# A pair's softmax issued one map of one head at a time, and a second gate group without set units

## The chip, the cores and the metric

The kernel runs on one core of one Trainium2 chip. The metric is the device time of one execution in microseconds. The kernel before took 1107.42 us, the median of 3 runs.

## The reference, cut to what matters

One layer on 256 tokens with 2048 features, all in float32. The input is normalised, multiplied by a wide matrix `w_in`, and the columns of the product feed two token mixers: gated linear attention (4 heads) and differential attention (16 heads with two softmax maps each). Both results are gated, sent through a branch matrix, merged, and projected out.

```python
h = rmsnorm(x, pre_norm_g[l])
proj = h @ w_in[l]                      # 2048 x (many columns)
(a_q, a_k, a_v, a_g, a_lr, b_q, b_k, b_v, b_g, m_a, m_b) = jnp.split(proj, offsets, axis=-1)
...
o_a = rmsnorm(gla_chunked(a_q, a_k, a_v, gk), gla_norm_g[l]) * silu(a_g)     # 4 heads, 512 wide
y_a = o_a @ w_branch_a[l]
...
# differential attention, per head: two maps of 256 x 256
s = jnp.einsum('bqhmd,bkhmd->bhmqk', qi, k)
p = jax.nn.softmax(jnp.where(mask, s, -jnp.inf), axis=-1)
w = p[:, :, 0] - lam * p[:, :, 1]
o = jnp.einsum('bhqk,bkhv->bqhv', w, v)
...
y_b = (rmsnorm(o_b, diff_norm_g[l]) * (1.0 - lam_init) * silu(b_g)) @ w_branch_b[l]
merged = sigmoid(m_a) * y_a + sigmoid(m_b) * y_b
x = x + rmsnorm(merged @ w_out[l], post_norm_g[l])
```

## The kernel before, in words

**Weights.** All weight matrices are cut into units of 128x1024 float32 (0.5 MB). A unit is loaded into one of 6 buffers called `raw`, or into a long-lived buffer called `chain` in which the POOL queue's DMAs add a second block of weights onto the first. ACT then writes a rounded copy `hi` (L341, for set units L304), DVE writes the rest `lo = raw - hi` (L342, L305), and PE multiplies: x's high part with hi, x's low part with hi, x's high part with lo. There are 3 `hi` and 3 `lo` buffers, and ACT and DVE prepare a unit up to `AHEAD = 4` steps before PE takes it.

**Set units and regular units.** Nine pairs of column groups are computed together as seven products in place of eight (p1, q3, p5, p2, q6, q7, p4; each of 4 units). These 9 x 28 = 252 units are the set units: 6 matmuls each at L712. When the product p5 is complete, ACT copies its PSUM bank into the tile `p` (L729) before the next product, q6, may write on in that bank. Everything else is regular: a unit of a gate group (`ag0` to `ag3` belong to the gated linear attention) has 12 matmuls at L512, a half of a channel chunk (`dq`, `dk`: queries and keys of the differential attention) has 16 at L533 and L535.

**The order of the steps** is written by hand in `schedule()`. `regular(keys)` appends the units of those column groups alone; `mixed(n, keys)` spreads n set units evenly between them. So `mixed(6, "ag2")` puts 6 set units among the 8 units of the third gate group, and `mixed(26, *channels(0))` puts 26 among the 16 units of the first four differential heads, which is called the first head stage. The group `m12` near the end is a merge gate with 14 set units.

**Background work.** Small work is written as generators, which `pump()` advances by one step: after a unit of some groups, after a channel chunk, and after every second set unit. `gla_out(hf, gates)` computes the output of two linear-attention heads: it fetches the values of the next head (`fetch_values`, L994, tiles `vh` and `vl`, from device memory on the SP queue), multiplies (9 matmuls per head at L494), normalises, and transposes. `diff_attention()` treats the 16 differential heads in 8 pairs. For a pair, `pair_scores` writes the scores of both heads and both maps into four PSUM banks. `exponents` then does one head: four masked maxima on DVE (L1041), one multiply that scales them (L1042), four exponentials on ACT (L1047). `diff_weights` joins the two maps, and later steps transpose the weights, apply them to the values, and normalise. DVE and ACT run these instructions in one order with the splits into hi and lo.

In the trace the trailing numbers and digits of the names are cut: `raw_ag` is a raw unit of any gate group, `raw_dq` and `raw_dk` of a channel chunk, `raw_s` of a set unit that is loaded plainly, `bg` a PSUM bank of background work, `set` one of a set product, `mm` one of a regular unit.

Of the kernel before, what the change touches and what calls it, by code (L numbers as in the profile page):

```python
# [10 lines left out]
AF = mybir.ActivationFunctionType  # L11
ALU = mybir.AluOpType
AX = mybir.AxisListType

P = 128
# [12 lines left out]
CUTS = ((0, P), (P, 3 * P))  # L28
# [47 lines left out]
def units(kind):  # L76
    return 2 * KT // ROWS[kind]


def schedule():  # L80

    kinds = {key: kind for key, kind, _, _ in chunk_plan()}
    steps = []
    blocks = [(i, n) for i in range(len(SETS)) for n in range(SLOTS * 4)]

    def regular(*keys):
        steps.extend((key, n) for key in keys for n in range(units(kinds[key])))

    def mixed(n, *keys):
        at = len(steps)  # L90
        regular(*keys)
        r = steps[at:]
        del steps[at:]
        for i, step in enumerate(r):
            steps.extend(blocks[: (i + 1) * n // len(r) - i * n // len(r)])
            del blocks[: (i + 1) * n // len(r) - i * n // len(r)]
            steps.append(step)

    def channels(g):
        return [key for key in kinds if key[:2] in ("dq", "dk") and key[2] == str(g)]  # L100

    order = [key for key, _, _, _ in chunk_plan()]
    def alone(n):
        steps.extend(blocks[:n])
        del blocks[:n]

    regular(*order[: order.index("v4")])
    mixed(SLOTS * 4, *order[order.index("v4") : order.index("ag0")])
    regular("ag0")
    mixed(4, "ag1")  # L110
    mixed(6, "ag2")
    mixed(26, *channels(0))
    mixed(28, *channels(1))
    mixed(28, *channels(2))
    mixed(28, *channels(3))
    mixed(14, "m12")
    mixed(42, *(f"y0{g}" for g in range(4)))
    alone(4)
    mixed(16, "y10", "y11")
    regular("y12", "y13")  # L120
    mixed(SLOTS * 4, "o2")
    regular("o3")
    assert not blocks
    return steps
# [41 lines left out]
def hybrid_kernel(ctx: ExitStack, tc, xt, xn, preg, postg, w, w2, gkb, glag, lamv, diffg, ident_d, causal_d, lmask_d, out):  # L166
    nc = tc.nc
    pe, act, dve, pool, sp = nc.tensor, nc.scalar, nc.vector, nc.gpsimd, nc.sync
# [14 lines left out]
    def sm(shape, name, dtype=F32, bufs=2):  # L183
        count[0] += 1
        return small.tile(shape, dtype, tag=name, name=f"{name}_{count[0]}", bufs=bufs)

    def t2(shape, name):
        count[0] += 1
        return small.tile(shape, F32, tag="t2", name=f"{name}_{count[0]}", bufs=8)

    def ps(tag):
        count[0] += 1
        return psum.tile([P, 512], F32, tag="bank", name=f"{tag}_{count[0]}")
# [5 lines left out]
    def f32(ap):  # L199
        return ap.bitcast(F32)  # L200


    steps = schedule()
    kinds, sizes, begins = {}, {}, {}
    off = 0
# [226 lines left out]
    neg_scale = const.tile([P, 2, 2], F32, name="neg_scale")  # L432
    score_scale = const.tile([P, 2], F32, name="score_scale")
# [392 lines left out]
    for g, n in enumerate(VG[2:]):  # L826
        banks = token_major(f"v{g + 2}", n, x_ops, 2)
# [169 lines left out]
    for g in range(3):  # L997
# [3 lines left out]
        banks = token_major(f"ag{g}", 512, x_ops)  # L1001
# [19 lines left out]
    def pair_scores(g, pair, qk):  # L1021
        banks = [[ps("bg"), ps("bg")] for _ in range(2)]
        for b in range(2):
            lo, up = CUTS[b]
            t, n = slice(P * b, P * b + P), up - lo
            for i2 in range(2):
                for m in range(2):
                    r = slice(64 * m, 64 * m + 64)
                    pe.matmul(banks[i2][m][:, lo:up], qk[r, 0, i2, t], qk[r, 1, i2, :n], start=True, stop=True)
        return [{"g": g, "pair": pair, "h": 2 * pair + i2, "banks": banks[i2]} for i2 in range(2)]  # L1030

    def exponents(s):
        cm = causal.rearrange("p a t -> p (a t)")
        prob = [t2([P, 384], f"prob{m}") for m in range(2)]
        mx = sm([P, 4], "mx", bufs=3)
        z = sm([P, 4], "z", bufs=4)
        banks = s["banks"]
        for m in range(2):
            for b in range(2):
                lo, up = CUTS[b]  # L1040
                dve.tensor_tensor_reduce(out=prob[m][:, lo:up], in0=banks[m][:, lo:up], in1=cm[:, lo:up], scale=1.0, scalar=-3e38, op0=ALU.add, op1=ALU.max, accum_out=mx[:, 2 * m + b : 2 * m + b + 1])  # L1041
        dve.tensor_tensor(out=mx, in0=mx, in1=neg_scale.rearrange("p m b -> p (m b)"), op=ALU.mult)  # L1042
        for m in range(2):
            for b in range(2):
                lo, up = CUTS[b]
                i = 2 * m + b
                act.activation(prob[m][:, lo:up], prob[m][:, lo:up], AF.Exp, scale=score_scale[:, b : b + 1], bias=mx[:, i : i + 1], accum_out=z[:, i : i + 1])  # L1047
        s.update(z=z, prob=prob)

    def diff_weights(s):  # L1050
        z, prob = s["z"], s["prob"]
        c = sm([P, 2], "c", bufs=2)
        dve.reciprocal(out=c, in_=z[:, 2:4])
        dve.scalar_tensor_tensor(out=c, in0=z[:, 0:2], scalar=neg_lam, in1=c, op0=ALU.mult, op1=ALU.mult)
        for b in range(2):
            lo, up = CUTS[b]
            dve.scalar_tensor_tensor(out=prob[0][:, lo:up], in0=prob[1][:, lo:up], scalar=c[:, b : b + 1], in1=prob[0][:, lo:up], op0=ALU.mult, op1=ALU.add)

    def turn_weights(s):
        bank = ps("bg")  # L1060
        for i in range(3):
            pe.transpose(bank[:, P * i : P * i + P], s["prob"][0][:, P * i : P * i + P], ident)  # L1062
        s["bank"] = bank
# [23 lines left out]
    def diff_attention():  # L1087

        last = pair = og = None
        n = 0  # L1090
        while "out1" not in done:
            yield
        while n < 16 or last or pair:
            new = None
            if n < 16:
                if n % 2 == 0:
                    while not waiting or f"pair{waiting[0][0]}{waiting[0][1]}" not in done:
                        yield
                    new, second = pair_scores(*waiting.pop(0))
                    exponents(new)  # L1100
                    yield
                    diff_weights(new)
                    exponents(second)
                    yield
                else:
                    new = second
                    diff_weights(new)
                    yield
                n += 1
                yield  # L1110
                turn_weights(new)
            while last and f"set{last['g']}" not in done:
                yield
            if last:
                weigh(last)
            if pair:
                bank = ps("bg")
                for i in range(2):
                    for b in range(2):
                        pe.transpose(bank[:, P * (2 * i + b) : P * (2 * i + b) + P], pair[1][:, i, b, :], ident)  # L1120
                s = pair[0]
                hi = obh[s["g"]][:, 2 * s["pair"] : 2 * s["pair"] + 2, :].rearrange("p h t -> p (h t)")
                lo = obl[s["g"]][:, 2 * s["pair"] : 2 * s["pair"] + 2, :].rearrange("p h t -> p (h t)")
            if new:
                new["wt"] = t2([P, 384], "wt")
                act.activation(new["wt"], new["bank"][:, :384], AF.Copy)
            if pair:
                split_out(bank, hi, lo, diffg_s)
                if pair[0]["pair"]:
                    g = pair[0]["g"]  # L1130
                    for t, far in ((obh[g], obh_far[g]), (obl[g], obl_far[g])):
                        pool.dma_start(far, f32(t))
                pair = None
            if last:
                if last["h"] % 2 == 0:
                    og = t2([P, 2, 2, P], "ogb")
                normed(last, og)
                if last["h"] % 2:
                    pair = (last, og)
            last = new  # L1140
            if n == 16:
                yield
                yield
# [26 lines left out]


    tasks.append(diff_attention())
    diff_heads(0)
    diff_heads(1)
# [21 lines left out]
    banks = token_major("m12", 512, x_ops, 2)  # L1196
# [4 lines left out]
    for g in range(4):  # L1201
        if g == 3:
            tasks.append(fetch_b())
        banks = token_major(f"y0{g}", 512, a_ops)
# [47 lines left out]
    low, up = slice(0, P), slice(P, S)  # L1252
# [97 lines left out]
    for g in range(4):  # L1350
        banks = token_major(f"y1{g}", 512, b_ops, 4)
# [53 lines left out]
    for g in (2,):  # L1405
        banks = token_major(f"o{g}", 512, m_ops)
# [10 lines left out]
    bank = ps("mm")  # L1417
# [8 lines left out]
    for c in range(2):  # L1426
        bank = ps("mm")
        for kt in range(KT):
            lo = 512 * (kt % 2) + 256 * c
# [68 lines left out]
```

## Time and profile before

| | |
|---|---|
| three runs | 1109.17, 1106.28, 1107.42 us; median 1107.42 |
| the profiled execution | 1110.03 us; its span in the profile 1108.2 us |
| mean granted TensorE clock in it | 0.994 |
| instructions | 15525 |
| DMA | 297.66 MB, mean 269 GB/s |

The profile is of one execution, not of the median one, so a sum over its rows is made against 1110.03 us. PE is TensorE's matmuls, PEld its weight loads, DVE is VectorE, ACT ScalarE, POOL GpSimd; SP only issues DMAs. A row of a group ends with the idle time of its engine just before its instructions, and with what ended most of it. In a timeline, the bracket at a row's end says how long the engine had idled before it and for whom. PEclk is the clock granted to TensorE as a share of the full one.

### The profile page before, as it was taken

Reading aid. Unit: us, or ns where it says so; the run is one execution under the profiler, and the core shown is the slowest. Engines: PE = TensorE matmul, PEld = TensorE weight load, DVE = VectorE, ACT = ScalarE, POOL = GpSimd, SP = SyncE. Lnnn points to the kernel's source line nnn. Section 1 sums busy time; section 2 is a strip of 40 time slices with the busy share of each in tenths; the row PEclk is TensorE's granted clock in tenths of the full one; section 3 lists DMA queues with packets and bytes.
Section 4 is the critical chain, followed back from the end, with each engine's and each line's share of the span. In section 5 each row is a group of like instructions: output and inputs, shape, how many; then the busy total and the mean of one; then the engine's idle time right before and its main releaser. Section 6 shows DMA issues by size and latency. Waiting matters only on the chain. (4 is left out here: it accounts for less than half of the span.)

```text
span 1108.2 us, 15525 instructions
## 1 busy us (share of the span) xinstructions
PE 1085.6 (98%) x5480; PEld 925.9 (84%) x5480; DVE 879.0 (79%) x1211; ACT 708.6 (64%) x1023; POOL 217.9 (20%) x315
## 2 busy tenths in 40 slices
PE   9999999999899999999999999899999999999997
PEld 8999888888788888888888888688887888888886
DVE  7787669998578889887887788968677687787994
ACT  8777456655566677675776767566565665546772
POOL 0213101211131222123213122113111222301100
PEclk9999999999999999999999999999999999999999
DMA  8889988599899988579979998869986999987874
GB/s 321 268 311 318 301 268 213 195 402 303 228 283 329 309 237 226 174 212 275 264 260 256 283 265 228 219 206 375 292 219 224 328 342 356 343 333 227 212 191 149
DMA packets 84990, 297.66 MB, mean 269 GB/s; under 512 B 10224, under 2 KB 11248, under 8 KB 84912
## 3 DMA queue, kind: packets, MB, share of 16 engines
q0 software_dynamic: 37984, 137.38, 47.2%
q1 hardware_dynamic: 46064, 158.02, 39.6%
q10 hardware_dynamic: 864, 1.27, 0.3%
q8 instruction: 43, 0.70, 0.2%
q14 instruction: 35, 0.29, 0.1%
HBM read 272.51 MB, written 24.12 MB: 268 GB/s over the span
## 5 line engine op out<-in xcount | busy, mean ns | idle before, releaser
L305 DVE TENSOR_TENSOR lo<-chain,hi 128x1024 fp32r<-128x1024 f32 x212 | 257.4, 1223 | 72.6 <-ACT hi L304 72.1
L304 ACT ACTIVATE hi<-chain 128x1024 fp32r<-128x1024 f32 x212 | 223.5, 1058 | 130.6 <-PE set L712 48.7
L533 PE MATMUL mm<-xs,hi 128*128 128x512 f32 x768 | 199.3, 392 | 3.5 <-ACT hi L341 3.5
L232 POOL DMA_DIRECT2D chain<-in_w_dram x112 | 97.4, 870 | 435.4 <-DVE lo L305 292.3
L533 PEld LDWEIGHTS mm<-xs,hi 128*128 128x128 f32 x768 | 142.6, 188 | 32.8 <-ACT hi L341 5.6
L712 PE MATMUL set<-hi,square 128*128 128x512 f32 x512 | 142.3, 399 | 4.0 <-ACT p L729 4.0
L512 PE MATMUL mm<-hi,xs 128*128 128x512 f32 (+2 forms) x512 | 119.3, 372 | 1.0 <-ACT hi L341 1.0
L712 PEld LDWEIGHTS set<-hi,square 128*128 128x128 f32 x512 | 95.1, 192 | 23.6 <-ACT p L729 4.6
L535 PEld LDWEIGHTS mm<-xs,lo 128*128 128x128 f32 x768 | 104.5, 190 | 9.0 <-DVE lo L342 1.7
L535 PE MATMUL mm<-xs,lo 128*128 128x256 f32 x768 | 107.3, 282 | 0.6 <-DVE lo L342 0.6
L712 PE MATMUL set<-hi,xs 128*128 128x512 f32 x384 | 105.3, 395 | 0.6 <-ACT hi L304 0.6
L512 PEld LDWEIGHTS mm<-hi,xs 128*128 128x128 f32 x512 | 94.8, 188 | 12.1 <-ACT hi L341 1.6
L341 ACT ACTIVATE hi<-raw_y 128x1024 fp32r<-128x1024 f32 x64 | 67.9, 1061 | 55.2 <-PE mm L512 31.7
L342 DVE TENSOR_TENSOR lo<-raw_y,hi 128x1024 fp32r<-128x1024 f32 x64 | 78.3, 1224 | 28.6 <-ACT hi L341 27.7
L712 PEld LDWEIGHTS set<-hi,xs 128*128 128x128 f32 x384 | 69.8, 188 | 14.4 <-ACT hi L304 1.1
L712 PE MATMUL set<-lo,square 128*128 128x512 f32 x256 | 80.0, 394 | 0.0
L233 POOL DMA_DIRECT2D chain<-in_w_dram x72 | 39.5, 563 | 151.3 <-DVE lo L305 134.4
L512 PE MATMUL mm<-lo,xs 128*128 128x512 f32 (+2 forms) x256 | 64.7, 369 | 0.0
L712 PE MATMUL set<-lo,xs 128*128 128x512 f32 x192 | 59.4, 390 | 0.1
L712 PEld LDWEIGHTS set<-lo,square 128*128 128x128 f32 x256 | 48.8, 191 | 11.1 <-DVE lo L305 0.2
L342 DVE TENSOR_TENSOR lo<-raw_dk,hi 128x1024 fp32r<-128x1024 f32 x32 | 39.1, 1222 | 22.7 <-ACT hi L341 22.7
L341 ACT ACTIVATE hi<-raw_dk 128x1024 fp32r<-128x1024 f32 x32 | 33.9, 1058 | 30.9 <-PE mm L533 29.3
(304 smaller groups left out, 1987.0 us busy)
## 6 DMA issues: line engine op xcount, KB each, us to landing
chain<-in_w_dram POOLq DMA_DIRECT2D x184, 512.0 KB, 9.1
raw_y<-in_w_dram SPq DMA_DIRECT2D x64, 512.0 KB, 7.7
raw_dq<-in_w_dram SPq DMA_DIRECT2D x32, 512.0 KB, 6.4
raw_dk<-in_w_dram SPq DMA_DIRECT2D x32, 512.0 KB, 6.6
raw_v<-in_w_dram SPq DMA_DIRECT2D x31, 416.0 KB, 5.5
raw_ag<-in_w_dram SPq DMA_DIRECT2D x24, 512.0 KB, 7.1
raw_s<-in_w_dram SPq DMA_DIRECT2D x20, 512.0 KB, 7.9
raw_k<-in_w_dram SPq DMA_DIRECT2D x16, 512.0 KB, 6.9
```

Source lines behind the costliest of these rows:

```text
L232: return pool.dma_start(dst, src, accum_op=ALU.add)
L233: return queue.dma_start(dst, src)
L304: act.activation(hi_t, raw, AF.Copy)
L305: dve.tensor_tensor(out=lo_t, in0=raw, in1=f32(hi_t), op=ALU.subtract)
L341: act.activation(hi_t[:, a:b], r, AF.Copy)
L342: dve.tensor_tensor(out=lo_t[:, a:b], in0=r, in1=f32(hi_t[:, a:b]), op=ALU.subtract)
L512: i = pe.matmul(banks[g][b][:, :n], a[part][:, P * b : P * b + P], w[:, c : c + n], start=first, stop=last)
L533: i = pe.matmul(o, hi[:, c], x_pair(kt), start=kt == 0, stop=kt == KT - 1)
L535: i = pe.matmul(o[:, :S], lo[:, c], x_ops(kt)[0], start=False, stop=False)
L712: i = pe.matmul(bank, a[part], wt[:, 512 * j : 512 * j + 512], start=go, stop=end, skip_group_check=not first)
```

## The change

Two things are changed. First, `exponents` takes one map of one head instead of both maps, and `diff_attention` calls it in four steps per pair: a pair goes through seven background steps where it went through five. The maxima are scaled by one multiply per map (128x2) where there was one per head (128x4): 32 multiplies in all where there were 16. Second, in `schedule()` the second gate group `ag1` loses its 4 set units; the third, `ag2`, gets 8 where it had 6, and the first head stage 28 where it had 26. The total stays 36.

```diff
@@ schedule()
-    regular("ag0")
-    mixed(4, "ag1")
-    mixed(6, "ag2")
-    mixed(26, *channels(0))
+    regular("ag0", "ag1")
+    mixed(8, "ag2")
+    mixed(28, *channels(0))
@@ exponents
-    def exponents(s):
+    def exponents(s, m):
         cm = causal.rearrange("p a t -> p (a t)")
-        prob = [t2([P, 384], f"prob{m}") for m in range(2)]
-        mx = sm([P, 4], "mx", bufs=3)
-        z = sm([P, 4], "z", bufs=4)
-        banks = s["banks"]
-        for m in range(2):
-            for b in range(2):
-                lo, up = CUTS[b]
-                dve.tensor_tensor_reduce(out=prob[m][:, lo:up], in0=banks[m][:, lo:up], ...)
-        dve.tensor_tensor(out=mx, in0=mx, in1=neg_scale.rearrange("p m b -> p (m b)"), op=ALU.mult)
-        for m in range(2):
-            for b in range(2):
-                act.activation(prob[m][:, lo:up], prob[m][:, lo:up], AF.Exp, ...)
-        s.update(z=z, prob=prob)
+        if m == 0:
+            s.update(mx=sm([P, 4], "mx", bufs=3), z=sm([P, 4], "z", bufs=4), prob=[])
+        bank, mx, z, prob = s["banks"][m], s["mx"], s["z"], t2([P, 384], f"prob{m}")
+        s["prob"].append(prob)
+        c = slice(2 * m, 2 * m + 2)
+        for b in range(2):
+            lo, up = CUTS[b]
+            dve.tensor_tensor_reduce(out=prob[:, lo:up], in0=bank[:, lo:up], ...)
+        dve.tensor_tensor(out=mx[:, c], in0=mx[:, c], in1=neg_scale[:, m], op=ALU.mult)
+        for b in range(2):
+            act.activation(prob[:, lo:up], prob[:, lo:up], AF.Exp, ...)
@@ diff_attention
                     new, second = pair_scores(*waiting.pop(0))
-                    exponents(new)
+                    exponents(new, 0)
+                    yield
+                    exponents(new, 1)
                     yield
                     diff_weights(new)
-                    exponents(second)
+                    exponents(second, 0)
                     yield
                 else:
                     new = second
+                    exponents(new, 1)
+                    yield
                     diff_weights(new)
                     yield
```

On ACT in the stage of `m12`, the last pair's exponentials, `hi` copies of set units (`chain`) and the copy `p` of p5's bank stand in this order before:

```order
L304 ACTIVATE hi_6910<-chain_177_2325 128x1024
L1047 ACTIVATE prob_599_6939,z_6942<-prob_599_6939,mx_6941,score_scale 128x128
L1047 ACTIVATE prob_599_6939,z_6942<-prob_599_6939,mx_6941,score_scale 128x256
L1047 ACTIVATE prob_600_6940,z_6942<-prob_600_6940,mx_6941,score_scale 128x128
L1047 ACTIVATE prob_600_6940,z_6942<-prob_600_6940,mx_6941,score_scale 128x256
L304 ACTIVATE hi_6952<-chain_178_2326 128x1024
L1047 ACTIVATE prob_604_6967,z_6970<-prob_604_6967,mx_6969,score_scale 128x128
L1047 ACTIVATE prob_604_6967,z_6970<-prob_604_6967,mx_6969,score_scale 128x256
L1047 ACTIVATE prob_605_6968,z_6970<-prob_605_6968,mx_6969,score_scale 128x128
L1047 ACTIVATE prob_605_6968,z_6970<-prob_605_6968,mx_6969,score_scale 128x256
L729 ACTIVATE p_608_6980<-set_6856 128x512
```

and in the changed kernel in this one:

```order
L1045 ACTIVATE prob_601_6955,z_6954<-prob_601_6955,mx_6953,score_scale 128x128
L303 ACTIVATE hi_6924<-chain_197_2515 128x1024
L1045 ACTIVATE prob_601_6955,z_6954<-prob_601_6955,mx_6953,score_scale 128x256
L1045 ACTIVATE prob_602_6971,z_6954<-prob_602_6971,mx_6953,score_scale 128x128
L303 ACTIVATE hi_6961<-chain_198_2516 128x1024
L1045 ACTIVATE prob_602_6971,z_6954<-prob_602_6971,mx_6953,score_scale 128x256
L728 ACTIVATE p_603_6977<-set_6870 128x512
L1045 ACTIVATE prob_607_7026,z_7025<-prob_607_7026,mx_7024,score_scale 128x128
L1045 ACTIVATE prob_607_7026,z_7025<-prob_607_7026,mx_7024,score_scale 128x256
```

Between the first `hi` copy and the copy `p` stood eight exponentials and one other `hi`; now three exponentials and one `hi` stand there, one exponential moved ahead, and the second head's follow the copy.

On ACT in a head stage, where a pair meets the plainly loaded set units (`raw_s`) and the next channel chunk (`raw_dq`), before:

```order
L304 ACTIVATE hi_5996<-raw_s_13_5994 128x1024
L1047 ACTIVATE prob_521_6031,z_6034<-prob_521_6031,mx_6033,score_scale 128x128
L1047 ACTIVATE prob_521_6031,z_6034<-prob_521_6031,mx_6033,score_scale 128x256
L1047 ACTIVATE prob_522_6032,z_6034<-prob_522_6032,mx_6033,score_scale 128x128
L1047 ACTIVATE prob_522_6032,z_6034<-prob_522_6032,mx_6033,score_scale 128x256
L304 ACTIVATE hi_6047<-raw_s_14_6045 128x1024
L1047 ACTIVATE prob_527_6063,z_6066<-prob_527_6063,mx_6065,score_scale 128x128
L1047 ACTIVATE prob_527_6063,z_6066<-prob_527_6063,mx_6065,score_scale 128x256
L1047 ACTIVATE prob_528_6064,z_6066<-prob_528_6064,mx_6065,score_scale 128x128
L1047 ACTIVATE prob_528_6064,z_6066<-prob_528_6064,mx_6065,score_scale 128x256
L729 ACTIVATE p_531_6076<-set_5935 128x512
```

and after:

```order
L303 ACTIVATE hi_6006<-raw_s_13_6004 128x1024
L1045 ACTIVATE prob_523_6043,z_6042<-prob_523_6043,mx_6041,score_scale 128x128
L1045 ACTIVATE prob_523_6043,z_6042<-prob_523_6043,mx_6041,score_scale 128x256
L303 ACTIVATE hi_6052<-raw_s_14_6050 128x1024
L1045 ACTIVATE prob_525_6063,z_6042<-prob_525_6063,mx_6041,score_scale 128x128
L1045 ACTIVATE prob_525_6063,z_6042<-prob_525_6063,mx_6041,score_scale 128x256
L728 ACTIVATE p_526_6069<-set_5945 128x512
L340 ACTIVATE hi_6073<-raw_dq_1_6071 128x1024
L1045 ACTIVATE prob_530_6125,z_6124<-prob_530_6125,mx_6123,score_scale 128x128
```

The `hi` of the channel chunk (`raw_dq`) had all eight exponentials of the pair ahead of it and now has four.

On the SP queue at the end of the third gate group (the last units of `ag2`, and the fetch of the second linear head's values), before:

```order
L320 DMA raw_ag_5_2995<-in_w_dram 128x1024
L320 DMA raw_ag_6_3041<-in_w_dram 128x1024
L320 DMA raw_ag_7_3071<-in_w_dram 128x1024
L994 DMA vh_2876<-vh_far_130 128x1024
L994 DMA vl_2877<-vl_far_134 128x1024
L320 DMA raw_dq_0_3107<-in_w_dram 128x1024
```

and after:

```order
L319 DMA raw_ag_5_2978<-in_w_dram 128x1024
L319 DMA raw_ag_6_3007<-in_w_dram 128x1024
L993 DMA vh_2822<-vh_far_130 128x1024
L993 DMA vl_2823<-vl_far_134 128x1024
L319 DMA raw_ag_7_3049<-in_w_dram 128x1024
L319 DMA raw_dq_0_3077<-in_w_dram 128x1024
```

The fetch moved ahead of one raw load. On PE, between the last product of the first linear head and the first one of the second stood a set unit and a gate unit; in the changed kernel these rows show only a set unit there:

```order
L493 MATMUL bg_2827<-vl_2601,ath_1802 128x512
L493 MATMUL bg_2827<-vh_2600,atl_1803 128x512
L711 MATMUL set_2791<-hi_2739,xs_73 128x512 x4
L711 MATMUL set_2791<-lo_2740,xs_73 128x512 x2
L493 MATMUL bg_2858<-vh_2822,ath_1802 128x512
L493 MATMUL bg_2858<-vl_2823,ath_1802 128x512
```

The second head's products moved ahead by one gate unit against the first head's.

More of the change, by code (lines that the diff above doesn't have):

```diff
@@ L1030, in pair_scores @@
         return [{"g": g, "pair": pair, "h": 2 * pair + i2, "banks": banks[i2]} for i2 in range(2)]
-    def exponents(s):
+    def exponents(s, m):
         cm = causal.rearrange("p a t -> p (a t)")
-        prob = [t2([P, 384], f"prob{m}") for m in range(2)]
-        mx = sm([P, 4], "mx", bufs=3)
-        z = sm([P, 4], "z", bufs=4)
-        banks = s["banks"]
-        for m in range(2):
-            for b in range(2):
-                lo, up = CUTS[b]
-                dve.tensor_tensor_reduce(out=prob[m][:, lo:up], in0=banks[m][:, lo:up], in1=cm[:, lo:up], scale=1.0, scalar=-3e38, op0=ALU.add, op1=ALU.max, accum_out=mx[:, 2 * m + b : 2 * m + b + 1])
-        dve.tensor_tensor(out=mx, in0=mx, in1=neg_scale.rearrange("p m b -> p (m b)"), op=ALU.mult)
-        for m in range(2):
-            for b in range(2):
-                lo, up = CUTS[b]
-                i = 2 * m + b
-                act.activation(prob[m][:, lo:up], prob[m][:, lo:up], AF.Exp, scale=score_scale[:, b : b + 1], bias=mx[:, i : i + 1], accum_out=z[:, i : i + 1])
-        s.update(z=z, prob=prob)
+        if m == 0:
[5 more added lines that the diff above has]
+            lo, up = CUTS[b]
+            dve.tensor_tensor_reduce(out=prob[:, lo:up], in0=bank[:, lo:up], in1=cm[:, lo:up], scale=1.0, scalar=-3e38, op0=ALU.add, op1=ALU.max, accum_out=mx[:, 2 * m + b : 2 * m + b + 1])
+        dve.tensor_tensor(out=mx[:, c], in0=mx[:, c], in1=neg_scale[:, m], op=ALU.mult)
+        for b in range(2):
+            lo, up = CUTS[b]
+            i = 2 * m + b
+            act.activation(prob[:, lo:up], prob[:, lo:up], AF.Exp, scale=score_scale[:, b : b + 1], bias=mx[:, i : i + 1], accum_out=z[:, i : i + 1])
     def diff_weights(s):
```

## The prediction

> **What bounds the kernel now.** I read the page's busy line first, then PE's waits, then the timeline and the windows around the two longest waits.
>
> ```profile
> span 1108.2 us, 15525 instructions
> PE 1085.6 (98%) x5480; PEld 925.9 (84%) x5480; DVE 879.0 (79%) x1211; ACT 708.6 (64%) x1023; POOL 217.9 (20%) x315
> ```
>
> PE is busy for 98% of the span, and the change takes no matmul away. It can only win what PE loses: waits, and matmuls run at a lowered clock. PE's waits (engine, line, waited for: total us, times, longest):
>
> ```profile
> PE set L712 <- ACT p L729: 4.0, 1, 4.0
> PE mm L533 <- ACT hi L341: 3.5, 5, 0.9
> PE bg L494 <- DMA vl<-vl_far: 3.0, 1, 3.0
> ...
> PE mm L535 <- DVE lo L342: 0.6, 2, 0.4
> ```
>
> Three losses lie where the change reaches: one 4.0 us wait for the copy `p`, one 3.0 us wait for a linear head's values, and seven short ones in the head stages (3.5 + 0.6 = 4.1 us). The windows around the two long waits show that each also lowers the clock (columns: window, length, busy of PE, PEld, DVE, ACT, POOL, then PEclk):
>
> ```profile
> 295.10:298.50 3.40, 0.37 (x3) 0.32 (x3) 0.94 (x1) 0.00 (x0) 0.89 (x1) 1.00 0.99 255
> 298.50:302.00 3.50, 3.50 (x10) 2.73 (x9) 0.03 (x1) 1.38 (x4) 0.00 (x0) 0.51 0.90 178
> 715.50:718.40 2.90, 0.04 (x1) 0.00 (x0) 2.69 (x9) 2.90 (x10) 0.00 (x0) 1.00 0.99 264
> 718.40:725.20 6.80, 5.64 (x13) 4.46 (x14) 2.36 (x5) 3.07 (x6) 0.00 (x0) 0.50 0.09 25
> ```
>
> After the first wait, 3.50 us of busy PE ran at 0.51: 3.50 x 0.49 = 1.7 us lost. After the second, 5.64 us ran at 0.50: 2.8 us lost. In reach are thus 3.0 + 1.7, 4.0 + 2.8, and 4.1: 15.6 us.
>
> **Term 1, the values of the second linear head.**
>
> ```profile
> 281.85 5.32 SPq L320 DMA_DIRECT2D raw_ag<-in_w_dram  x2
> 289.93 0.33 SPq L994 DMA_DIRECT2D vh<-vh_far  x1
> 290.35 0.38 SPq L994 DMA_DIRECT2D vl<-vl_far  x1
> ...
> 285.20 1.98 PE L512 MATMUL mm<-hi,xs 128*128 128x512 f32 x8
> 287.92 0.39 PE L494 MATMUL bg<-vh,ath 128*128 128x512 f32 x1
> 289.96 1.07 PE L712 MATMUL set<-hi,square 128*128 128x512 f32 x4
> 291.32 0.84 PE L512 MATMUL mm<-hi,xs 128*128 128x512 f32 x3
> ...
> 298.14 0.50 PE L494 MATMUL bg<-vl,ath 128*128 128x512 f32 x1 [3.03 <-DMA vl<-vl_far]
> ...
> DMA to landing us min/median/max: 7.7/7.7/7.7
> ```
>
> The fetch goes out at 289.93, at the very moment the first head's products end (289.96): its tiles take the buffers that those products read. `vl` lands 7.7 us after its issue (the row of that tile), and PE stands until 298.14. In the changed order the fetch takes buffers of tiles that are long dead (the transposed queries and keys of the linear heads), and stands on SP behind `raw_ag_6` and ahead of `raw_ag_7`. `raw_ag_6` went out at 281.85, and PE began the gate unit behind which the first head follows at 285.20, 3.35 us later. From there to the second head's first use of `vl` lie the gate unit (285.20 to 287.92: 2.72), the first head (287.92 to 289.96: 2.04) and one set unit (289.96 to 291.32: 1.36). The issues of the raw and of `vh` ahead of it cost two steps of 0.4 (289.93 to 290.35), so `vl` would have 3.35 - 0.8 + 2.72 + 2.04 + 1.36 = 8.7 us. In the denser group DVE, whose split sets `raw_ag_6` free, runs nearer to PE; I take 0.2 to 0.7 off for that: 8.0 to 8.5 us, against a landing of 7.7. All fetches of this line spread more:
>
> ```profile
> DMA to landing us min/median/max: 3.3/6.4/11.3
> ```
>
> Full gain 4.7; none, if it lands as late against PE as before. I take 4.0, since the time given exceeds this transfer's own row; the other 0.7 is left for a short wait for `vl` and for the second head's transposes, which now come one gate unit sooner behind their normalisation on DVE. The bounds are 0 and 4.7.
>
> **Term 2, the copy of p5's bank in the stage of m12.**
>
> ```profile
> 712.40 1.06 ACT L304 ACTIVATE hi<-chain 128x1024 fp32r<-128x1024 f32 x1 [2.48 <-PE set L712]
> 713.72 0.50 ACT L1047 ACTIVATE prob<-prob,mx,score_scale 128x128 f32<-128x128 f32 x1 [0.27 <-DVE mx L1042]
> 714.22 0.58 ACT L1047 ACTIVATE prob<-prob,mx,score_scale 128x256 f32<-128x256 f32 x1
> 715.87 1.04 ACT L304 ACTIVATE hi<-chain 128x1024 fp32r<-128x1024 f32 x1
> 716.81 0.48 ACT L1047 ACTIVATE prob<-prob,mx,score_scale 128x128 f32<-128x128 f32 x1
> 718.93 0.57 ACT L729 ACTIVATE p<-set 128x512 f32<-128x512 f32 x1
> ...
> 712.97 0.42 DVE L1041 CUSTOM_DVE_ANT_0 prob<-bg,causal 128x256 f32<-128x256 f32 x1
> 713.52 0.16 DVE L1042 TENSOR_TENSOR mx<-mx,neg_scale 128x4 f32<-128x4 f32 x1
> ...
> 714.47 1.07 PE L512 MATMUL mm<-lo,xs 128*128 128x512 f32 x4
> 719.55 0.80 PE L712 MATMUL set<-hi,square 128*128 128x512 f32 x1 [4.02 <-ACT p L729]
> ```
>
> PE stops at 715.53 and the copy starts only at 718.93: from 713.72 ACT works through four exponentials (2.15), a `hi` (0.94) and four more (2.12). Now the first multiply needs two maxima, not four, and stands third from the front on DVE: it can go where the fourth maximum went, at 712.97 and not at 713.52, so the first exponential starts near 713.2, ahead of the `hi` of 712.40. The new order then has .50 + .95 + .58 + .50 + .95 + .58 = 4.06 us ahead of the copy: it starts at 717.3, or up to 717.8 if DVE's second map is late, and PE resumes about 0.6 behind it (as 718.93 to 719.55), at 717.9. The wait becomes 2.4 in place of 4.0: 1.6 saved. Does the clock still fall? It fell after a 3.03 us wait, and the longest of the waits that left it up is:
>
> ```profile
> 627.55 1.21 PE L533 MATMUL mm<-xs,hi 128*128 128x512 f32 x4 [0.91 <-ACT hi L341]
> ...
> 616.00:702.00 86.00, 84.60 (x464) 71.43 (x463) 70.14 (x133) 60.89 (x108) 18.11 (x23) 1.00 0.91 259
> ```
>
> 0.91 us, within a window whose PEclk is 1.00, left it up. 2.4 lies between 0.91 and 3.03. The record that halved it covers 3.40 us with 0.37 of work; a wait of 2.4 leaves at least 1.0 us of work in any such stretch, nearly three times that. I take the clock as kept: 1.6 + 2.8 = 4.4, bounds 1.6 (it halves all the same) and 6.8 (nothing left).
>
> [...]
>
> **Term 3, the head stages.**
>
> ```profile
> 622.90 1.04 ACT L304 ACTIVATE hi<-raw_s 128x1024 fp32r<-128x1024 f32 x1
> 623.85 0.48 ACT L1047 ACTIVATE prob<-prob,mx,score_scale 128x128 f32<-128x128 f32 x1
> 625.97 0.58 ACT L729 ACTIVATE p<-set 128x512 f32<-128x512 f32 x1
> 626.45 1.04 ACT L341 ACTIVATE hi<-raw_dq 128x1024 fp32r<-128x1024 f32 x1
> ```
>
> The pair's second four exponentials (623.85 to 625.97: 2.1 us) stand ahead of the copy and of the `hi` for which PE then waits 0.91 us at 627.55 (it was ready at 626.64). Now they stand behind it, so that `hi` starts near 624.3. Each of the seven waits is under 0.92, so each is covered. I take 3.7 of 4.1, leaving a rest where another late `hi` takes the place; bounds 0 and 4.1.
>
> **What it adds.** The multiplies:
>
> ```profile
> L1042 DVE TENSOR_TENSOR mx<-mx,neg_scale x16: 157/161/164, 410.1 to 715.8; 128x4 f32<-128x4 f32 x16
> L305 DVE TENSOR_TENSOR lo<-chain,hi 128x1024 fp32r<-128x1024 f32 x212 | 257.4, 1223 | 72.6 <-ACT hi L304 72.1
> ```
>
> Sixteen more by 0.161 = 2.6 us of DVE over eight pairs (one of half the width at the same price). DVE has 70.14 of 86.00 us in the stage above, so PE's work hides it: nothing. Without this cover it would cost 2.6. Two extra steps per pair delay the pair by two pumps; eleven pumps come per pair and the last pair's scores keep their place on PE, so the end doesn't move: nothing. The moved set units keep their matmuls, DMAs and splits; the load of the next raw passes behind the fetch, and a regular `ag1` only relaxes DVE. In the third group it tightens:
>
> ```profile
> 268.00:300.00 32.00, 28.97 (x133) 23.94 (x132) 22.70 (x29) 16.40 (x23) 5.12 (x6) 0.98 0.99 286
> 330.00:360.00 30.00, 30.00 (x168) 26.16 (x167) 25.01 (x30) 19.16 (x25) 5.29 (x8) 1.00 1.04 335
> ```
>
> Two more set units there are 2 x 1.22 = 2.4 us on DVE against 2 x 1.36 = 2.7 on PE: 25.1 of 31.7 us. DVE keeps 6.6 us of room, and the first head stage shows 25.01 of 30.00 with PE never idle: nothing.
>
> **Sum.** 4.0 + 4.4 + 3.7 = 12.1 us. The profiled execution took 1110.03, so it would take 1097.9; its time is 2.6 above the median of the runs, 1107.42, from which the same sum gives 1095.3. I say 1097.0, between the two. A difference under 0.3% (3.3 us, a time over 1104.1) can't be told from no change.
>
> **Rivals.** (A) The clock still halves at m12: term 2 is 1.6, the sum 9.3, the time 1099.8. For it: the border lies unseen between 0.91 and 3.03 us. Against: only part of a record would be idle. (B) The values land late all the same: the fetch competes with denser chain loads (the 268 to 300 window has its DMA engines busy for 0.99), and at 11.3 us, the longest landing of its line, PE waits up to 3.2 us and loses the 1.7 of clock again: term 1 is about 0, the time 1101. (C) The waits only change place: the first is replaced by the second head's transposes waiting for DVE, the second gives 1.6, the third half: 1.6 + 2 = 3.6, the time near 1104. (D) Slower: the score banks. A pair's four PSUM banks are freed by the maxima, which now run in four steps rather than two. If PE's next product needs one of them before the last step has run, it waits up to a set unit (1.36 us) or more, once per pair. Eight pairs at 1.36 are 10.9 us and would only eat the gain; it is slower by 3.3 from (12.1 + 3.3) / 8 = 1.9 us per pair on, and at 2.3 per pair the time is 1113. Against it: none of PE's waits today, those left out above included, is for the maxima. That the change doesn't do what it says is no rival: the order of the instructions shows it done.
>
> **How the numbers follow.** The sum as taken 0.43; A 0.22; B 0.12; C 0.16, a quarter of it still faster by over 0.3%; D 0.07. Faster: 0.43 + 0.22 + 0.12 + 0.04 = 0.81; within 0.3%: 0.12; slower: 0.07. All gains in full give 1107.4 - 15.6 = 1091.8, so the range begins at 1091; it ends at 1105, where C's low end leaves about 2.4 us of gain.
>
> **What would show it.** Term 1: no 3 us wait for `vl` near 295 us, and PEclk 1.00 behind it. Term 2: one PE wait for `p` of about 2.4 us in the m12 stage; PEclk above 0.9 behind it says the clock held, 0.5 says rival A. Term 3: the rows of L533 and L535 for `hi` and `lo` down to a few tenths. Wrong would be a new PE wait for a PSUM bank or for a DVE row in the first head stage, or a fetch that still lands behind PE's need.

## The result and the profile after

The changed kernel took 1098.22 us (median of 4 runs, 1096.99 to 1099.29) beside 1107.19 us for the kernel before (4 runs): ratio 0.9916, 95% interval 0.9899 to 0.9934. The forecast was 1097.0 with a range of 1091.0 to 1105.0. The profiled execution of the changed kernel took 1099.29 us, 10.7 us less than that of before; the sum had said 12.1.

The page's first lines and PE's waits, after:

```profile
span 1097.5 us, 15541 instructions
PE 1083.4 (99%) x5480; PEld 926.3 (84%) x5480; DVE 879.0 (80%) x1227; ACT 708.2 (65%) x1023; POOL 214.5 (20%) x315
```

```profile
PE set L711 <- ACT p L728: 2.3, 1, 2.3
PE bg L426 <- DVE ones L423: 1.1, 1, 1.1
PE mm L511 <- ACT hi L340: 1.0, 1, 1.0
PE bg L1121 <- DVE ogb L1082: 0.7, 1, 0.7
PE bg L493 <- DMA vl<-vl_far: 0.4, 1, 0.4
```

PE is still busy for 99% of the span. The waits for `p` and `vl` shrank from 4.0 and 3.0 us to 2.3 and 0.4, the rows of the head stages for `hi` and `lo` (3.5 and 0.6 us) are gone, and one row is new: 0.7 us for `ogb`.

The next windows run between the same steps of the program in both kernels: from the first `lo` matmul of the second head stage to that of the third, and from there to the start of the last `lo` row of the fourth. Before, then after (window, length, busy of PE with its number of matmuls, PEld, DVE, ACT, POOL, then PEclk, the DMA engines' share and GB/s):

```profile
421.98:516.81 94.83, 93.53 (x511) 78.79 (x509) 83.73 (x153) 65.17 (x117) 24.37 (x33) 1.00 0.80 224
516.81:698.84 182.03, 179.24 (x979) 151.53 (x978) 147.37 (x275) 126.85 (x221) 43.49 (x55) 1.00 0.94 261
```

```profile
419.61:512.72 93.11, 93.06 (x511) 78.35 (x509) 83.28 (x162) 66.37 (x121) 23.88 (x32) 1.00 0.80 224
512.72:690.87 178.15, 178.15 (x978) 151.83 (x977) 146.16 (x283) 126.56 (x221) 40.68 (x55) 1.00 0.95 269
```

The same matmuls now take 1.72 and 3.88 us less, 5.6 us together. That is more than the 4.1 us of listed waits. A listed wait runs from the modelled end of one matmul to the start of the next, and single matmuls of 0.39 us start 0.23 us apart in a row (287.92 and 288.15 us in the kernel before), so, by an estimate from these two numbers, a wait costs some 0.16 us more than its row says; for seven waits that is 1.1 us, most of the rest.

The m12 stage after, on ACT and PE:

```profile
705.20 0.50 ACT L1045 ACTIVATE prob<-prob,mx,score_scale 128x128 f32<-128x128 f32 x1 [3.25 <-DVE mx L1041]
705.69 1.05 ACT L303 ACTIVATE hi<-chain 128x1024 fp32r<-128x1024 f32 x1
...
708.65 0.59 ACT L1045 ACTIVATE prob<-prob,mx,score_scale 128x256 f32<-128x256 f32 x1
709.23 0.57 ACT L728 ACTIVATE p<-set 128x512 f32<-128x512 f32 x1
...
709.86 1.77 PE L711 MATMUL set<-hi,square 128*128 128x512 f32 x4 [2.29 <-ACT p L728]
```

The copy starts 709.23 - 705.20 = 4.03 us after the first exponential (4.06 was worked out), and PE waited 2.29 us (2.4 was worked out).

### The profile page after: what moved, and what is told of

The parts are those of the page before. It is cut to its first block, busy times and chain, and to the rows that moved or that the text cites. A ratio compares the mean times of both kernels' runs of the same rounds, so it can differ in the third digit from the quotient of the medians.

```text
span 1097.5 us, 15541 instructions
## 1 busy us (share of the span) xinstructions
PE 1083.4 (99%) x5480; PEld 926.3 (84%) x5480; DVE 879.0 (80%) x1227; ACT 708.2 (65%) x1023; POOL 214.5 (20%) x315
## 4 chain that ended last, share of the span: by engine, by line
PE 94%; DVE 2%; issue 1%; DMA 1%; ACT 1%; POOL 0%; SPq 0%; DVEq 0%; POOLq 0%; ACTq 0%
PE set L711 31%; PE mm L511 31%; PE mm L532 16%; PE mm L534 8%; PE bg L511 2%; PE mm L493 1%; PE bg L897 1%; PE bg L1028 1%; DMA vl<-vl_far 1%; PE bg L493 1%; PE bg L1059 0%; DVE lo L341 0%; PE bg L1242 0%; DMA raw_first<-in_w_dram 0%; PE bg L1121 0%
## 5 line engine op out<-in xcount | busy, mean ns | idle before, releaser
L511 PEld LDWEIGHTS mm<-lo,xs 128*128 128x128 f32 x256 | 48.0, 189 | 5.6 <-DVE lo L341 0.3
```

What stands on the lines that cost most here:

```text
L511: i = pe.matmul(banks[g][b][:, :n], a[part][:, P * b : P * b + P], w[:, c : c + n], start=first, stop=last)
```

## The experiments

Each kernel is compared with the kernel before on one chip; gains in us are medians.

**The two parts apart.** One kernel has the new `exponents` and the old `schedule()` (called the split here), one the reverse (the schedule alone), and the changed kernel ran again beside them.

```diff
 # split_alone: the changed kernel, with
-    regular("ag0", "ag1")
-    mixed(8, "ag2")
-    mixed(28, *channels(0))
+    regular("ag0")
+    mixed(4, "ag1")
+    mixed(6, "ag2")
+    mixed(26, *channels(0))
 # schedule_alone: the kernel before, with the reverse of this
```

Expected of the split alone:

> The softmax split with the schedule of before. Theory (the two parts work at different places and add up): the wait for the linear head's values near 295 us stays at about 3.0 us with the half clock behind it; the wait for the copy p in the m12 stage is 2.3 us as in the changed kernel; the seven waits of the head stages (4.1 us) are gone. Gain 1.7 at the wait, 1.1 to 2.8 of clock, 4.1 in the head stages, less the new 0.7 us wait for ogb: 6.2 to 7.9 us, ratio 0.993 to 0.9945. Rival (the head stages' waits went because the set units stand at other places): they stay, and the gain is 2 to 4 us, ratio 0.9965 to 0.998.

Of the schedule alone:

> The new places of the set units with the old softmax. Theory: the wait for vl falls from 3.0 to 0.4 us and the clock holds there, 4.3 us in all, ratio 0.996; the m12 wait stays at 4.0 us with two half-clock records, and the head stages' seven waits stay (4.1 us). Rival (the head stages' waits go with the schedule): 8 us, ratio 0.9925.

Of the changed kernel beside them:

> The changed kernel on the same chip as its parts. If the parts add up, its gain is the sum of those of split_alone and schedule_alone, 10 to 12 us by the profiles; by the runs so far 9 us, ratio 0.9916. The record with the half clock behind the m12 wait is there or not from run to run (mean clock 0.996 or 0.998), which is worth 1.7 us.

Measured against 1106.87 us before: the split alone 1101.81 us (ratio 0.9956, 0.9944 to 0.9969), the schedule alone 1106.97 us (1.0000, 0.9991 to 1.0009), both 1098.76 us (0.9934, 0.9921 to 0.9946). The split alone is short of what was expected, the schedule alone wins nothing where 0.996 was expected, and both together are short of the 9 us of the first runs; yet the schedule is worth 3.0 us behind the split: the parts do not add up. Each alone has a bad place that the two together lack. With the new schedule and the old softmax, a pair's eight exponentials stand in one row on ACT ahead of the `hi` of a channel chunk:

```profile
433.37 0.48 ACT L1046 ACTIVATE prob<-prob,mx,score_scale 128x128 f32<-128x128 f32 x1
...
437.04 0.59 ACT L1046 ACTIVATE prob<-prob,mx,score_scale 128x256 f32<-128x256 f32 x1
437.62 1.04 ACT L340 ACTIVATE hi<-raw_dq 128x1024 fp32r<-128x1024 f32 x1
...
438.71 1.89 PE L532 MATMUL mm<-xs,hi 128*128 128x512 f32 x7 [1.73 <-ACT hi L340]
```

In this profile PE waited 1.73 us behind 4.2 us of exponentials (433.37 to 437.62) and that `hi`; the kernel before has no wait in this pair. With the split and the old schedule a `lo` is late instead, behind set and softmax work on DVE:

```profile
474.57 1.22 PE L535 MATMUL mm<-xs,lo 128*128 128x256 f32 x8 [0.90 <-DVE lo L342]
```

The changed kernel has neither wait. The schedule shifts when the background steps of the pairs fall among the units. The second head stage, between the same two rows as above, with the schedule alone and then with the split alone:

```profile
418.63:514.86 96.23, 93.62 (x511) 79.02 (x509) 83.00 (x150) 65.60 (x117) 22.95 (x32) 1.00 0.78 218
```

```profile
420.49:516.36 95.87, 94.89 (x513) 79.93 (x512) 84.02 (x163) 66.75 (x122) 23.04 (x32) 1.00 0.80 220
```

It takes 94.83 us in the kernel before, so each part alone loses there (1.4 and 1.0 us) and both together win 1.7. In the third and fourth head stages the schedule makes no difference: 182.02 us with the schedule alone, 178.15 with the split alone, as in the kernels before and after. So the split alone and both together are 2.8 us apart in the second head stage. Some of that is work that falls into this stage with the one and elsewhere with the other: three more weight loads and their matmuls, at most 0.7 us (an estimate at 0.23 us each). So 2.1 us or more of the 3.0 lie here. The late `lo` is 0.9 of them; the rest is longer busy time (94.89 against 93.06 us) and was not followed further.

**Is the 3.0 us wait for `vl` the kernel's own?** The kernel before was profiled once more.

> The kernel before once more, for a second profile of it. Theory (the landing of the values differs from execution to execution, and the profile read for the prediction held a late one): the wait for vl near 295 us is 0.5 to 2 us and no half-clock record follows it; the m12 wait is 4.0 us again and the seven waits of the head stages are the same to 0.1 us. Rival (the 3.0 us wait is the kernel's own): it is 3.0 us again with the half clock behind it.

It took 1106.83 us. SP's issue of `vl`, its landing and PE's two waits in this second execution:

```profile
291.94 0.38 SPq L994 DMA_DIRECT2D vl<-vl_far  x1
...
DMA to landing us min/median/max: 5.4/5.4/5.4
...
296.04 0.70 PE L494 MATMUL bg<-vh,ath 128*128 128x512 f32 x2 [0.23 <-DMA vh<-vh_far]
297.43 0.50 PE L494 MATMUL bg<-vl,ath 128*128 128x512 f32 x1 [0.23 <-DMA vl<-vl_far]
```

`vl` landed in 5.4 us where the first profile had 7.7, PE waited 0.23 twice, and the clock held (the next single matmuls took 0.39 to 0.40 us each, up to 0.63 in the first profile). The m12 wait (4.02 us) and the seven short waits were the same to 0.1 us. So the 3.0 us and the 1.7 us of clock behind them are not in every execution; the first profile had caught the slowest of the three. How often they come, two profiles can't say. The theory holds, with waits even shorter than the 0.5 us that it began at.

**The buffers alone.** The kernel before, with only the destination of this fetch changed:

```diff
+    spent = parts["n2"]
     store_squares()
 ...
-        vh[h], vl[h] = u([P, 2, 512], "vh", F32R), u([P, 2, 512], "vl", F32R)
+        if h == 1:
+            vh[h], vl[h] = (t.rearrange("p (b k) t -> p b (k t)", b=2) for t in spent)
+        else:
+            vh[h], vl[h] = u([P, 2, 512], "vh", F32R), u([P, 2, 512], "vl", F32R)
```

> The kernel before, except that the second linear head's values go into two tiles that are long dead (a set operand's, n2) and not into the first head's buffers; schedule and softmax are those of before. Theory (the fetch was late because its buffers were still read): the fetch goes out some us before the first head's products, the wait for vl is gone or under 0.5 us and the clock holds: 4.2 to 4.7 us, ratio 0.9957 to 0.9962, as much as the whole move of the set units. Rival (it is the move of the set units as such, the fetch being slow among dense loads): the fetch still lands too late, a wait of 1 us or more stays, gain under 2 us.

1105.20 us, ratio 0.9990 (0.9981 to 0.9999): 1.1 us by the ratio, 1.7 by the medians. The waits for the fetch were gone in its profile; it has a 0.7 us wait for the head's normalisation (`ua`), which is 0.5 in the second profile of before. The mechanism is as expected, the size is not (4.2 to 4.7 us expected); that fits the second profile of before. The same edit behind the split:

> The softmax split with the schedule of before, and the second linear head's values in the two long-dead tiles. split_alone took 1101.8 us and the changed kernel 1098.8 on one chip: the move of the set units is worth 3.0 us behind the split, though nothing alone. Theory (the fetch is 1.5 to 2 us of it, the rest is a late lo near 474 us that only the old schedule has): ratio 0.9935 to 0.9945, the vl wait gone, the 0.9 us wait near 474 us still there. Rival (all of it is the fetch): ratio 0.9925 to 0.993.

1101.63 us, 0.9952 (0.9939 to 0.9964), against 1101.81 (0.9956) for the split alone in another set of runs: no difference that can be told, and less than both ranges expected. Its waits for the fetch were gone (1.1 us in `split_alone`), the `ua` wait rose to 0.8, and the 0.9 us wait for `lo` stayed. So most of the 3.0 us that the schedule adds behind the split is not this fetch, which agrees with the times of the second head stage above; no run takes the late `lo` away by itself.

**The p5 copy alone.** One instruction moves from ACT to DVE, in the kernel before and in the changed one:

```diff
                 kept = st(name)
-                act.activation(kept, bank, AF.Copy)
+                if (n, name) == (5, "p5"):
+                    dve.tensor_copy(kept, bank)
+                else:
+                    act.activation(kept, bank, AF.Copy)
```

> The kernel before, except that one copy of p5's bank, that of the set in the m12 stage, is done by DVE, where it stands behind the last maxima, and not by ACT behind eight exponentials. Theory (that copy's place alone makes the m12 loss): the wait falls from 4.0 to about 1.3 us, no half clock, and the units behind it wait 0 to 1 us for hi: gain 3.5 to 5.5 us, ratio 0.995 to 0.997. Rival (PE would have stood there for the hi of the next units all the same): the wait only changes its name, gain under 1.5 us.

> The changed kernel with the same single copy on DVE. Theory (what is left of the m12 loss is that copy behind four exponentials and two hi): the wait of 2.3 us falls under 0.7 us, no half-clock record in any run: 1.6 to 3.3 us faster than the changed kernel, ratio 0.9905 to 0.992 against before. Rival: hi and lo of the next units are late, under 0.8 us gained.

In the kernel before: 1100.31 us, 0.9945 (0.9932 to 0.9958), 6.4 us where 3.5 to 5.5 were expected. In the changed one: 1094.55 us, 0.9892 (0.9877 to 0.9906), also more than expected. The copy and PE's wait, first in the kernel before with the edit, then in the changed one with it:

```profile
711.88 0.69 DVE L730 COPY p<-set 128x512 f32<-128x512 f32 x1
...
712.62 1.20 PE L712 MATMUL set<-hi,square 128*128 128x512 f32 x4 [0.84 <-DVE p L730]
```

```profile
702.90 0.68 DVE L729 COPY p<-set 128x512 f32<-128x512 f32 x1
...
703.64 1.20 PE L711 MATMUL set<-hi,square 128*128 128x512 f32 x4 [0.46 <-DVE p L729]
```

4.02 us became 0.84, 2.29 became 0.46, the clock held in both profiles (the four matmuls behind the copy took 1.20 us in each, 2.08 and 1.77 without the edit), and no later wait of that stage took their place. One copy's place is worth at least as much as the split as a whole (5.1 us), and what the change left of it is 2.7 to 4.6 us (0.9916 and 0.9934 less 0.9892, of 1107 us).

**Other places for the set units.** Both with the split:

```diff
 # ag1_four
-    regular("ag0", "ag1")
+    regular("ag0")
+    mixed(4, "ag1")
     mixed(8, "ag2")
-    mixed(28, *channels(0))
+    mixed(24, *channels(0))
 # ag2_six
-    mixed(8, "ag2")
-    mixed(28, *channels(0))
+    mixed(6, "ag2")
+    mixed(30, *channels(0))
```

> The softmax split; set units 4 in the second gate group, 8 in the third, 24 in the first head stage: the second group is as before, the third as changed. The fetch again takes the first head's buffers and stands behind the last raw of the group. Theory (what the fetch wins comes from the buffers, which the regular second group leaves free): waits of 0.5 to 3 us for vh and vl come back, ratio 0.9945 to 0.997. Rival (the denser third group does it): no such wait, ratio about 0.9925.

> The softmax split; no set units in the second gate group, 6 in the third, 30 in the first head stage: the second group as changed, the third as before. The fetch takes dead tiles, and one more gate unit (2.7 us) stands between the two heads on PE. Theory: no wait for vl at all, where the changed kernel had 0.4 to 1.9 us; the rest as the changed kernel: ratio 0.9905 to 0.993. Rival (30 set units in the first head stage are too dense for DVE and ACT): waits for hi and lo there of over 2 us, ratio 0.994 or more.

The first took 1105.89 us (0.9984, 0.9974 to 0.9993): waits of 2.2 us for `vh` and 1.8 for `vl` came back near 297 us, and one of 0.9 near 377, with the clock lowered behind the first: from 301.76 to 303.89 us single matmuls took 0.63 us, 0.39 ahead of the waits. The waits are those of the theory, but the time is above its range (0.9945 to 0.997): the profile is of the fastest of eleven executions, 1102.97 us, and what the others lost more has no profile. The second took 1108.35 us (1.0012, 1.0003 to 1.0021) and missed what both theories expected. There was no wait for the second head's values, but one of 1.1 us for `ua`; the third head's values came far too late:

```profile
349.02 0.45 SPq L993 DMA_DIRECT2D vh<-vh_far  x1
...
366.44 0.76 PE L493 MATMUL bg<-vh,ath 128*128 128x512 f32 x1 [5.95 <-DMA vh<-vh_far]
368.95 0.79 PE L493 MATMUL bg<-vl,ath 128*128 128x512 f32 x1 [1.75 <-DMA vl<-vl_far]
...
DMA to landing us min/median/max: 3.6/7.4/19.3
```

The slowest of these fetches, the third head's `vl`, took 19.3 us to land. Behind the two waits single matmuls took 0.63 us (369.54 to 371.67 us), and the mean clock of this execution was 0.993, where that of the changed kernel was 0.996. The landing alone is not the reason: in the changed kernel the same fetch lands after 17.0 us and PE doesn't wait for it. There PE takes `vh` 19.8 us after its issue (344.43 to 364.19); here it wanted it 366.44 - 5.95 - 349.02 = 11.5 us after. So in these runs the places of the set units decide how far ahead of their use the fetches go out, and the changed kernel's 0, 8 and 28 is the best of the four divisions that ran with the split.

**What is left, taken together.** The changed kernel with the copy on DVE, the fetch into the dead tiles, and the last steps of the attention left to the next stage:

```diff
-    while tasks:
-        pump()
+    with tc.issue_after(latest[0]):
+        while next(tasks[1], DONE) is not DONE:
+            pass
+    tasks.pop(1)
```

> The changed kernel with that copy on DVE, the second linear head's values in two long-dead tiles, and the differential attention's last steps not drained at the end of m12 but left to the pumps of the next stage. Theory (each takes one remaining wait: 2.3 us and its half clock, 0.4 to 1.9 us for vl, 0.7 us for ogb): 3 to 5.5 us faster than the changed kernel, ratio 0.9885 to 0.9905 against before. Rival: waits move to the transposes (ua, ogb) and no more than 2 us are won.

1093.78 us, 0.9883 (0.9867 to 0.9899): the fastest kernel of this study, though not to be told from the copy alone on DVE (1094.55). The waits for `ogb` and for the second head's values were gone; in this execution the third head's values came 1.0 us late at 364 us, and a `hi` came 1.7 us late at 9 us.

## Why the prediction was right, and where its sizes were off

**The bound.** Right: no matmul went away, and the gain is what PE had lost to waits and to the lowered clock.

**Term 1 was the wrong size: 4.0 us forecast, at most about 1 us found.** The step that failed is the first one, "Full gain 4.7", which took the wait and the half clock of one execution for the kernel's. The second profile of before has 0.46 us there in two waits, the buffers alone bring 1.1 us by the ratio (1.7 by the medians), and the schedule alone nothing. The lead was worked out well: `vl` was issued at 280.63 and wanted at 289.14 - 0.42 = 288.72, 8.1 us later (8.0 to 8.5 forecast). The landing was not: 8.5 us in one execution of the changed kernel, 10.0 in the next, where PE waited 1.90 us.

```profile
280.63 0.43 SPq L993 DMA_DIRECT2D vl<-vl_far  x1
...
DMA to landing us min/median/max: 8.5/8.5/8.5
...
289.14 0.51 PE L493 MATMUL bg<-vl,ath 128*128 128x512 f32 x1 [0.42 <-DMA vl<-vl_far]
```

```profile
DMA to landing us min/median/max: 10.0/10.0/10.0
...
290.11 0.50 PE L493 MATMUL bg<-vl,ath 128*128 128x512 f32 x1 [1.90 <-DMA vl<-vl_far]
```

The earlier issue did not keep the time to landing: it was 0.8 to 4.6 us longer than in the two profiles of before (7.7 and 5.4). The stretch was denser, with the DMA engines busy for 1.00 to 1.02 of 280 to 290 us in the changed kernel and for 0.87 of 290 to 295 and 0.96 of 295 to 298 us in the first profile of before; that this is the reason is not shown. A fetch that still lands behind PE's need is one of the signs of being wrong that the prediction names, and it came in both executions.

**Term 2 was right in its wait and half right in its clock: 4.4 forecast.** The wait came out at 2.29 us. The clock was taken as kept because a stretch of 3.40 us would still hold 1.0 us of work. No run shows that this much keeps it: in the profiled execution PE worked 1.12 of 3.41 us (706.84 to 710.25), and the clock stood at 0.50 from 710.25 to 713.66 us. These 3.41 us at 0.50 lost 1.7 us, so 1.7 + 2.8 - 1.7 = 2.8 us were won there. In the second execution it held (the four matmuls behind the wait took 1.20 us, 1.77 in the first), and 1.7 + 2.8 = 4.5 were won. Rival A and the sum as taken both happen, from one execution to the next.

**Term 3 was right, but too small: 3.7 forecast, 5.6 between the same steps.** All seven waits went, none came in their place. The listed waits, 4.1 us, were taken for the whole loss; by the estimate above each costs some 0.16 us more than its row, and in the second head stage the schedule had to help (1.7 us there, 3.9 in the two stages behind it).

**What it adds.** The multiplies cost what was said (a median of 156 ns each, 161 taken) and show in no wait of PE; DVE is busy for 83.28 + 146.16 of the 271.26 us of the windows above:

```profile
L1041 DVE TENSOR_TENSOR mx<-mx,neg_scale x32: 142/156/161, 403.1 to 722.5; 128x2 f32<-128x2 f32 x32
```

"The end doesn't move: nothing" was wrong by 0.7 us: the two extra steps make the last pair's transposes meet a normalisation that isn't done (the `ogb` row, which the split alone has too and the schedule alone hasn't). Nothing in the denser third gate group waits for DVE, as forecast.

**The sum.** 0 to 1 for term 1, 2.8 to 4.5 for term 2, 5.6 for term 3, less 0.7, make 7.7 to 10.4 us, against 8.1 and 9.0 measured in two sets of runs. That the forecast of 1097.0 lay only 1.2 us from the time is partly luck: term 1 was some 3 us or more too large and term 3 was 1.9 too small, and the time was set between the sum against the profiled execution and the one against the median; that last one, 1095.3, would have been 2.9 us off.

**The rivals.** (B), values that land late all the same, came in its mechanism: PE waited 0.42 and 1.90 us for `vl`, though the clock held (the next single matmuls took 0.39 to 0.40 us each), and the larger term 3 kept the time from 1101. (C), waits that only change place, holds in part for each part by itself (new waits of 0.9 and 1.73 us) but not for the two together. (D), the score banks: no wait of PE in any of these profiles is for the maxima.

## What to carry to other kernels

A wait for a DMA in one profile is one draw; before its length enters a sum, take a second profile of the same kernel, since in the two profiles of the kernel before the waits that come from the order of the engines repeat to 0.1 us (4.02 us twice for `p`) and those that come from landings don't (3.03 and 0.23 us for `vl`). Measure a gain between the same two steps of the program, as the listed waits leave some of it out (here 4.1 of 5.6 us were listed). Then search for a short instruction that frees a buffer of the bottleneck engine and stands in another engine's queue behind a batch of background work: here the place of one 0.57 us copy was worth 6 us, and moving it in the changed kernel beat both kernels. Two edits to an order written by hand don't add: measure them together and apart, since each shifts where the other's work falls.

## What the runs showed of the hardware

The same wait of 2.29 us, for `p` in the m12 stage, stands in six profiles. In three the clock fell behind it: in the changed kernel, `split_alone` and `split_other_buffers` a row of four set matmuls then took 1.77, 2.08 and 1.91 us. In three it held: in the changed kernel's second profile, `ag1_four` and `ag2_six` the four matmuls behind the wait took 1.20, 1.19 and 1.20 us. A stretch of 3.41 us that holds most of the wait and the next one, in the changed kernel, in `split_other_buffers` and in `ag1_four`:

```profile
706.84:710.25 3.41, 1.12 (x6) 0.62 (x5) 2.67 (x5) 3.41 (x11) 0.00 (x0) 1.00 1.01 292
710.25:713.66 3.41, 3.41 (x10) 2.64 (x9) 1.74 (x4) 1.68 (x4) 0.00 (x0) 0.50 0.90 280
```

```profile
710.07:713.48 3.41, 1.44 (x6) 1.22 (x7) 2.44 (x7) 3.19 (x9) 0.00 (x0) 1.00 1.05 271
713.48:716.89 3.41, 3.41 (x9) 2.66 (x9) 1.51 (x2) 1.91 (x2) 0.00 (x0) 0.50 0.74 281
```

```profile
711.65:715.06 3.41, 1.54 (x7) 0.94 (x5) 2.22 (x6) 3.41 (x9) 0.00 (x0) 1.00 1.03 302
715.06:718.47 3.41, 2.99 (x13) 2.50 (x14) 2.27 (x6) 2.88 (x7) 0.00 (x0) 1.00 1.03 314
```

PE worked 1.12, 1.44 and 1.54 us of the first stretches, and the second ones ran at 0.50, 0.50 and 1.00. The length of the wait alone doesn't decide it, since it is 2.29 us in all six profiles; what does is not shown. In the changed kernel's first profile the fall cost 3.41 x 0.50 = 1.7 us, in its second nothing.

Two executions of one kernel also differ ahead of the stages compared here. In the first profile of before the first product of the first linear head (`bg<-vh,ath`) begins at 287.92 us, in its second at 289.52, 1.6 us apart, so the spans of two single executions, set side by side, can hide or feign as much.
